# Relative-position rows spread in memory by one copy instead of four writes from SBUF

## The chip, the cores and the metric

The kernel runs on one core of a Trainium2 chip. The metric is the device time of one execution in microseconds (us). Lower is better.

## What is computed

One layer of a decoder trunk for 256 tokens of 2048 features: a normalisation, one combined projection into the queries, keys, values and gates of three token mixers (native sparse attention, stick-breaking attention, indexer-selected attention), their gated merge, a gated MLP with a causal convolution, a per-layer embedding gate, and a final normalisation. Of this the change touches only how the relative-position bias gets into SBUF. The reference adds a bias that depends on the distance of query and key to the logits of two of the mixers:

```python
def t5_bucket(dist):
    n = jnp.maximum(dist, 0)
    ...
    return jnp.where(n < max_exact, n, large)

bias = jnp.transpose(tab_gr[t5_bucket(dist)], (2, 3, 0, 1))
logits = jnp.einsum('bgrqd,bgkd->bgrqk', qb, kb).astype(jnp.float32) * scale + bias.astype(jnp.float32)
```

There are 12 heads with such a bias (8 and 4), and `tab` has 32 buckets for each.

## The kernel before

**Matrix products.** Weights come from memory in tiles of at most 1 MB, one DMA each on SP's queue, into the buffers `raw` (four). `load_w` (lines 114 to 129) makes two parts of each: `hi` on ACT (L125) and the rest `lo` on VectorE (L126), four buffers each, 1024 columns at a time. I call one such piece of work a split; it holds half of a weight tile. `gemm` (L137, L138) then runs a pair of matmuls for each of 16 blocks of 128 features, so a half tile is eight pairs. A feature tile (`feature_tiles`) is 16 pairs, ended by a fold: ACT copies half of the PSUM tile (L238), VectorE adds (L239), GpSimd scales (L240). A value tile (`value_tiles`, L290 to L292) takes four weight tiles.

**Foreground and background.** `tile_of` loads and splits the weights of the next tile before the epilogue of the last one is written down. The mixers are generators in the background: `pump()` advances each active generator by one `yield`, and takes up one waiting generator, after every feature tile (after every second weight tile of a value tile). The instruction order on each engine is then set by a scheduler from simulated times, so an instruction can stand earlier or later than its place in the program text. Every engine works its instructions off in order, and DMAs issued by an engine stand in that order too.

**The tile order around the change.** sbq (four feature tiles), sbk (four), sbv (one value tile of four weight tiles), then ikw, dckv, iq, dq and so on. `later(toeplitz())` stands behind sbq.

**The position rows.** `toeplitz` (lines 317 to 333) multiplies the table by a one-hot matrix (L319), which gives for each of 12 heads the 256 biases by distance, and writes them into `rrow`, 12 partitions of 384 numbers, the last 128 masked (L321, L322). A Toeplitz tile needs row p shifted by p. For this each head's row of 1536 bytes is written 128 times into the scratch tensor `scr` in memory, and `toe` reads it back with a step of 383 numbers from partition to partition, two heads in each of six DMAs (L330). The writes are four DMAs of three heads each, so out of three partitions (L326). Both are issued by ACT (`nc.scalar`). The stick-breaking part (`stick`) does not use `toe`; the first reader is `selected` (L440), after 240 us.

The parameters `prm` (L267) come in one DMA of 128 rows with 2508 numbers, 10,032 bytes each.

Of the kernel before, what the change touches and what calls it, by code (L numbers as in the profile page):

```python
# [11 lines left out]
F32 = mybir.dt.float32  # L12
F32R = mybir.dt.float32r

P = 128
S = 256
# [21 lines left out]
def trunk(ctx, tc, xT, pT, wf, wv, wg, wpa, wpb, wpc, wout, ck1, cv1, gmix, params, fg, fu, fd,  # L38
          plg, plp, out):
    nc = tc.nc  # L40
# [17 lines left out]
    def psa():  # L58
        return pa.tile([P, 512], F32, tag="pa", name="pa")
# [4 lines left out]
    def feat(name, dt=F32):  # L64
        return f2.tile([P, 512], dt, tag="f2", name=name)
# [4 lines left out]
    def tmp2(name):  # L70
        return wk.tile([P, 512], F32, tag="t2", name=name, bufs=4)

# [1 line left out]
    x_sb = big.tile([P, KT, S], F32, tag="x", name="x_sb")  # L74
    warm = cst.tile([P, 2], F32, tag="warm", name="warm")
    vec.memset(warm, 0.0)
# [33 lines left out]
    uk, uv, w2k, w2v = (par(n, 2) for n in ("wuk", "wuv", "ck2", "cv2"))  # L110
    cws = par("cw", NFF)

# [1 line left out]
    def load_w(src, cuts, cols):  # L114
        kt = sum(cuts)
        if first:
            raw = first.pop().rearrange("p (k c) -> p k c", c=cols)
        else:
            raw = wr.tile([P, 2048], F32, tag="raw", name="raw")[:, 0:kt * cols].rearrange("p (k c) -> p k c", c=cols)
            nc.sync.dma_start(raw, src)  # L120
        parts, k = [], 0
        for n in cuts:
            hi = wh.tile([P, 1024], F32R, tag="hi", name="hi")[:, 0:n * cols].rearrange("p (k c) -> p k c", c=cols)
            lo = wh.tile([P, 1024], F32R, tag="lo", name="lo")[:, 0:n * cols].rearrange("p (k c) -> p k c", c=cols)
            act(hi, raw[:, k:k + n, :], AF.Copy)  # L125
            vec.tensor_tensor(lo, raw[:, k:k + n, :], hi.bitcast(F32), op=ALU.subtract)  # L126
            parts.append((hi, lo, n))
            k += n
        return parts
# [43 lines left out]
            return r, rn, ps  # L173
        return spread

# [1 line left out]
    active, waiting = [], deque()  # L177

    def pump():
# [9 lines left out]
        while active or waiting:  # L189
            pump()  # L190

# [1 line left out]
    pending = []  # L193

    def flush():
# [13 lines left out]
    def later(*gens):  # L209
        then(lambda: waiting.extend(gens))  # L210

# [1 line left out]
    hs = []  # L213
    ssq4 = [tmp2("ssq4") for _ in range(2)]
    for k in range(KT):
# [27 lines left out]
    norm = []  # L243
# [3 lines left out]
    def feature_tiles(n, name):  # L247
        tiles = []

        def one(i):  # L250
            def evac(ps):
                if i % 2 == 0:
                    tiles.append(feat(name))
                fold_norm(tiles[-1][:, (i % 2) * 256:(i % 2) * 256 + 256], ps, norm[0])
                pump()

            def run(parts):
                ps = psg()
                gemm(ps, parts, hs)
                if norm:  # L260
                    evac(ps)
                    return
                early.append((evac, ps))
                if len(early) == 2:
                    early.insert(0, mixer_norm())
                elif len(early) == 4:
                    nc.sync.dma_start(prm, params)  # L267
                    norm.extend(early.pop(0)()[0:2])
                    for f, ps in early:
                        f(ps)  # L270
            return run

        for i in range(n):
            tile_of(wf[fidx[0]], (8, 8) if fidx[0] else (4, 4, 4, 4), 128, one(i))
            fidx[0] += 1
        return tiles
# [34 lines left out]
        split(o, ps[:, 0:256])  # L311
        return o

# [1 line left out]
    toes = []  # L315

    def toeplitz():
        pt = psa()
        mm(pt[0:12, 0:256], tabs, oh, start=True, stop=True)  # L319
        rrow = cst.tile([12, 384], F32, tag="rrow", name="rrow")  # L320
        nc.gpsimd.memset(rrow, NEG)  # L321
        vec.tensor_copy(rrow[:, 0:256], pt[0:12, 0:256])  # L322
        scr = nc.dram_tensor("scr", (12, P, 384), F32, kind="Internal").ap()
        yield
        for i in range(4):
            nc.scalar.dma_start(scr[3 * i:3 * i + 3], rrow[3 * i:3 * i + 3, None, :].to_broadcast([3, P, 384]))  # L326
            yield
        for i in range(6):
            t = feat("toe")
            nc.scalar.dma_start(t.rearrange("p (h k) -> p h k", h=2),  # L330
                                bass.AP(tensor=scr.tensor, offset=scr.offset + 127 + 2 * i * P * 384,
                                        ap=[[383, P], [P * 384, 2], [1, S]]))
            toes.append(t)

# [1 line left out]
    o_b, o_c, o_a = [], [], []  # L336

    def stick(h):
# [22 lines left out]
           skip_group_check=True)  # L361
        o_b.append(to_xs(ps, "ob"))

# [1 line left out]
    gates = cst.tile([P, 2, 24], F32, tag="gates", name="gates")  # L365
    wi = cst.tile([P, 2, 8], F32, tag="wi", name="wi")
    latent = {}
# [95 lines left out]
        if i == 1:  # L463
            o_c.append(to_xs(accs["c"], "oc"))

# [1 line left out]
    comp = {}  # L467

    def blocks(key, src, pe):
# [121 lines left out]
        if i == 1:  # L591
            o_a.append(to_xs(accs["a"], "oa"))

# [1 line left out]
    sbq = feature_tiles(4, "sbq")  # L595
    later(toeplitz())
    sbk = feature_tiles(4, "sbk")
    sbv = value_tiles(0, "sbv")
# [27 lines left out]
    then(drain)  # L626
    later(*(sparse(h, i) for h in range(8) for i in range(2)))

# [1 line left out]
    y, ys = [], []  # L630

    def gate_tile(parts):
# [66 lines left out]
    for n in range(KT):  # L699
        tile_of(wout[n], (8, 8), 128, lambda parts, n=n: out_tile(parts, n))  # L700

# [1 line left out]
    pre = {}  # L703

    def gate_up(parts, f):
# [102 lines left out]
    later(embed_inputs())  # L808
    ffn_down(NFF // CHUNK - 1, prev, True)

# [1 line left out]
    def ple_tile(parts, n):  # L812
        if n == 0:
            sums["f"] = wk.tile([P, S], F32, tag="ssq", name="ssq")
        pj = half(pps, n)
        ps = psg()
        if n == KT - 1:
            k = 0
            for hi, lo, c in parts:
                for j in range(c):  # L820
                    xh, xl = pxl[k][:, 0:256], pxl[k][:, 256:512]
                    for e, (w, x) in enumerate(((hi, xh), (hi, xl), (lo, xh))):
                        mm(ps[:, 0:256], w[:, j, :], x, start=k + e == 0, stop=k == KT - 1 and e == 2)  # L823
                    k += 1
            ple_evac(ps, pj, n)
            return
        gemm(ps, parts, pxl)
        if n == 0:
            sums["s"] = rstd_of([sums["q"]], D, "r1")
            sums["g"] = lambda: ple_evac(ps, pj, n)  # L830
            return
        if n == 1:
            sums["r"] = sums["s"]()[0]
            sums["g"]()
        ple_evac(ps, pj, n)
# [117 lines left out]
```

## Time and profile before

| | |
|---|---|
| median of 3 runs | 1672.39 us (1672.28 to 1672.94) |
| span of the profiled execution | 1670.0 us |
| TensorE busy | 1626.6 us, 97% of the span |
| VectorE, ACT, GpSimd busy | 68%, 53%, 10% |
| memory read / written | 299.94 MB / 4.46 MB |

The profiled execution's own time is not listed apart from its span; the median of the runs is 2.39 us longer than the span. The span runs from the first to the last instruction; PE is the matmul part of TensorE, PEld its weight load, DVE VectorE, POOL GpSimd, SP the engine that issues most DMAs; a q behind a name is the engine's own instruction queue. "Granted clock" is the share of TensorE's full clock.

### The profile page before, as it was taken

Reading aid. Unit: us, or ns where it says so; the run is one execution under the profiler, and the core shown is the slowest. Engines: PE = TensorE matmul, PEld = TensorE weight load, DVE = VectorE, ACT = ScalarE, POOL = GpSimd, SP = SyncE. Lnnn points to the kernel's source line nnn. Section 1 sums busy time; section 2 is a strip of 40 time slices with the busy share of each in tenths; the row PEclk is TensorE's granted clock in tenths of the full one; section 3 lists DMA queues with packets and bytes.
Section 4 is the critical chain, followed back from the end, with each engine's and each line's share of the span. In section 5 each row is a group of like instructions: output and inputs, shape, how many; then the busy total and the mean of one; then the engine's idle time right before and its main releaser. Section 6 shows DMA issues by size and latency. Waiting matters only on the chain.

```text
span 1670.0 us, 24647 instructions
## 1 busy us (share of the span) xinstructions
PE 1626.6 (97%) x9382; PEld 1418.8 (85%) x9382; DVE 1143.9 (68%) x1903; ACT 876.8 (53%) x1431; POOL 169.1 (10%) x177
## 2 busy tenths in 40 slices
PE   8499999999999999999999999999999999999996
PEld 6388888888888888888888888888888888889886
DVE  7145586776777666667777777666776677667775
ACT  5148455555565555555555555445554455446664
POOL 4001161210001110012100000000000000001122
PEclk7799999999999999999999999999999999999998
DMA  7265446554444555555555555565546655565551
GB/s 285 80 232 188 154 175 217 202 187 150 140 153 165 195 209 189 189 211 193 185 193 183 196 185 185 158 228 193 186 155 197 225 180 178 171 196 168 202 202 51
DMA packets 55074, 306.06 MB, mean 183 GB/s; under 512 B 5868, under 2 KB 9260, under 8 KB 27052
## 3 DMA queue, kind: packets, MB, share of 16 engines
q1 hardware_dynamic: 51552, 299.96, 52.2%
q10 hardware_dynamic: 3404, 4.52, 0.9%
q8 instruction: 74, 1.21, 0.3%
q14 instruction: 44, 0.36, 0.1%
HBM read 299.94 MB, written 4.46 MB: 182 GB/s over the span
## 4 chain that ended last, share of the span: by engine, by line
PE 95%; ACTq 2%; DVE 1%; ACT 0%; issue 0%; DVEq 0%
PE pg L137 58%; PE pg L138 29%; ACTq L326 2%; PE pg L292 1%; PE pg L290 1%; PE pg L291 1%; PE po L589 1%; PE po L501 0%; PE po L500 0%; PE po L585 0%; PE pg L823 0%; PE pa L543 0%; PE pa L544 0%; PE pa L576 0%; PE pa L154 0%; PE pa L412 0%
## 5 line engine op out<-in xcount | busy, mean ns | idle before, releaser
L126 DVE TENSOR_TENSOR lo<-raw,hi 128x1024 fp32r<-128x1024 f32 (+2 forms) x616 | 697.8, 1134 | 427.9 <-ACT hi L125 426.3
L125 ACT ACTIVATE hi<-raw 128x1024 fp32r<-128x1024 f32 (+2 forms) x616 | 602.3, 979 | 704.6 <-PE pg L137 455.8
L137 PE MATMUL pg<-h,hi 128*128 128x512 f32 x1328 | 482.6, 403 | 25.7 <-ACT hi L125 23.1
L137 PE MATMUL pg<-xf,hi 128*128 128x512 f32 x1408 | 488.7, 394 | 0.0
L138 PE MATMUL pg<-xf,lo 128*128 128x256 f32 x1408 | 389.9, 277 | 0.0
L138 PE MATMUL pg<-h,lo 128*128 128x256 f32 x1328 | 379.9, 286 | 3.7 <-DVE lo L126 3.6
L137 PEld LDWEIGHTS pg<-h,hi 128*128 128x128 f32 x1328 | 253.1, 191 | 87.0 <-ACT hi L125 24.1
L137 PEld LDWEIGHTS pg<-xf,hi 128*128 128x128 f32 x1408 | 264.0, 188 | 61.1
L138 PEld LDWEIGHTS pg<-xf,lo 128*128 128x128 f32 x1408 | 264.4, 188 | 0.1
L138 PEld LDWEIGHTS pg<-h,lo 128*128 128x128 f32 x1328 | 255.1, 192 | 8.0 <-DVE lo L126 6.3
L137 PE MATMUL pg<-f,hi 128*128 128x512 f32 x704 | 245.8, 394 | 0.0
L138 PE MATMUL pg<-f,lo 128*128 128x256 f32 x704 | 195.5, 278 | 0.0
L137 PEld LDWEIGHTS pg<-f,hi 128*128 128x128 f32 x704 | 132.1, 188 | 30.3
L678 POOL TENSOR_TENSOR ssq<-ssq,sqn 128x256 f32<-128x256 f32 x44 | 51.1, 1161 | 871.7 <-ACT sqn L677 867.2
L138 PEld LDWEIGHTS pg<-f,lo 128*128 128x128 f32 x704 | 132.4, 188 | 0.0
L137 PE MATMUL pg<-ys,hi 128*128 128x512 f32 x256 | 88.7, 393 | 0.0
L137 PE MATMUL pg<-xp,hi 128*128 128x512 f32 x240 | 83.8, 393 | 0.0
L240 POOL TENSOR_TENSOR gt<-fold,r 128x256 f32<-128x256 f32 x48 | 40.5, 845 | 358.7 <-DVE fold L239 336.7
L138 PE MATMUL pg<-ys,lo 128*128 128x256 f32 x256 | 70.8, 277 | 0.0
L138 PE MATMUL pg<-xp,lo 128*128 128x256 f32 x240 | 67.4, 281 | 0.0
L137 PEld LDWEIGHTS pg<-ys,hi 128*128 128x128 f32 x256 | 47.9, 187 | 11.0
L143 ACT ACTIVATE fold<-pg 128x256 f32<-128x256 f32 x151 | 55.1, 365 | 0.0
(257 smaller groups left out, 1675.2 us busy)
## 6 DMA issues: line engine op xcount, KB each, us to landing
raw<-in_wg_dram SPq DMA_DIRECT2D x48, 1024.0 KB, 4.8
raw<-in_fg_dram SPq DMA_DIRECT2D x44, 1024.0 KB, 4.9
raw<-in_fu_dram SPq DMA_DIRECT2D x44, 1024.0 KB, 4.8
raw<-in_fd_dram SPq DMA_DIRECT2D x64, 704.0 KB, 4.1
raw<-in_wf_dram SPq DMA_DIRECT2D x33, 1024.0 KB, 4.8
raw<-in_wout_dram SPq DMA_DIRECT2D x16, 1024.0 KB, 4.9
raw<-in_plg_dram SPq DMA_DIRECT2D x16, 1024.0 KB, 4.9
raw<-in_wv_dram SPq DMA_DIRECT2D x8, 1024.0 KB, 11.0
```

Of the source, the lines that this page charges most:

```text
L125: act(hi, raw[:, k:k + n, :], AF.Copy)
L126: vec.tensor_tensor(lo, raw[:, k:k + n, :], hi.bitcast(F32), op=ALU.subtract)
L137: mm(ps[:, 0:512], hi[:, j, :], xs[k][:, 0:512], start=k == 0, stop=last)
L138: mm(ps[:, 256:512], lo[:, j, :], xs[k][:, 0:256], start=False, stop=last, skip_group_check=True)
L143: act(t, ps[:, 256:512], AF.Copy)
L240: nc.gpsimd.tensor_tensor(dst, t, r, op=ALU.mult)
L290: mm(pss[t], xh, hi[:, j, :], start=k == 0, stop=False)
L291: mm(pss[t], xl, hi[:, j, :], start=False, stop=False)
L292: mm(pss[t], xh, lo[:, j, :], start=False, stop=k == KT - 1)
L326: nc.scalar.dma_start(scr[3 * i:3 * i + 3], rrow[3 * i:3 * i + 3, None, :].to_broadcast([3, P, 384]))
L589: mm(o, nv[c][:, b * 256 + g * 128:b * 256 + g * 128 + 128], pt_[:, s * 128:s * 128 + 128], start=False, stop=s == nb - 1)
L678: nc.gpsimd.tensor_tensor(ssq, ssq, t, op=ALU.add)
```

## The change

`scr` gets the layout (128, 12, 384) in place of (12, 128, 384). `rrow` is written once into a new tensor `row` in memory, 12 rows of 1536 bytes, and one DMA from memory to memory writes the 18,432 bytes of `row` 128 times into `scr`. The reads of `toe` have the same shape; a partition's row now lies 12 x 384 - 1 numbers behind that of the partition before. The generator has three yields ahead of the reads instead of five.

```diff
-        scr = nc.dram_tensor("scr", (12, P, 384), F32, kind="Internal").ap()
-        yield
-        for i in range(4):
-            nc.scalar.dma_start(scr[3 * i:3 * i + 3], rrow[3 * i:3 * i + 3, None, :].to_broadcast([3, P, 384]))
-            yield
+        row = nc.dram_tensor("row", (12, 384), F32, kind="Internal").ap()
+        scr = nc.dram_tensor("scr", (P, 12, 384), F32, kind="Internal").ap()
+        nc.scalar.dma_start(row, rrow)
+        yield
+        nc.scalar.dma_start(scr, row[None, :, :].to_broadcast([P, 12, 384]))
+        yield
+        yield
         for i in range(6):
             t = feat("toe")
             nc.scalar.dma_start(t.rearrange("p (h k) -> p h k", h=2),
-                                bass.AP(tensor=scr.tensor, offset=scr.offset + 127 + 2 * i * P * 384,
-                                        ap=[[383, P], [P * 384, 2], [1, S]]))
+                                bass.AP(tensor=scr.tensor, offset=scr.offset + 127 + 2 * i * 384,
+                                        ap=[[12 * 384 - 1, P], [384, 2], [1, S]]))
             toes.append(t)
```

From line 323 on the changed kernel's lines are numbered differently: the write of `row` is L325, the copy L327, the reads of `toe` L332 (L330 before).

Where these DMAs stand on ACT, in the stretch of the last sbq tiles. Before, the four writes of `scr`; a `hi<-raw` is a split, a `fold` the end of a feature tile, and DMAHW is a count of landed DMAs:

```order
L238 ACTIVATE fold<-pg 128x256 [waits PE_49]
L172 ACTIVATE r_360<-pa 128x256 [waits PE_49]
L326 DMA scr<-rrow 384x1x384 [waits DVE_49]
L326 DMA scr<-rrow 384x1x384
L326 DMA scr<-rrow 384x1x384 [waits DMAHW1_49]
L125 ACTIVATE hi<-raw 128x1024 [waits DMAHW3_49,PE_49,Activation_49]
L326 DMA scr<-rrow 384x1x384
L125 ACTIVATE hi<-raw 128x1024 [waits PE_49,Activation_49]
L238 ACTIVATE fold<-pg 128x256 [waits PE_49]
L125 ACTIVATE hi<-raw 128x1024 [waits DMAHW4_49,PE_49,Activation_49]
L125 ACTIVATE hi<-raw 128x1024 [waits DVE_49,PE_49]
```

and with the change:

```order
L238 ACTIVATE fold<-pg 128x256 [waits PE_49]
L172 ACTIVATE r_360<-pa 128x256 [waits PE_49]
L325 DMA row<-rrow 12x384 [waits DVE_49]
L125 ACTIVATE hi<-raw 128x1024 [waits DMAHW3_49,PE_49,Activation_49]
L125 ACTIVATE hi<-raw 128x1024 [waits PE_49,Activation_49]
L238 ACTIVATE fold<-pg 128x256 [waits PE_49]
L327 DMA scr<-row 128x4608 [waits DMAHW6_49]
L125 ACTIVATE hi<-raw 128x1024 [waits DMAHW4_49,PE_49,Activation_49]
L125 ACTIVATE hi<-raw 128x1024 [waits DVE_49,PE_49]
```

One small DMA stands in the place of the first three writes and none between the two splits; the copy follows behind the next fold and waits for the landing of `row`.

The reads of `toe` on ACT, before, at the end of the value tile:

```order
L125 ACTIVATE hi<-raw 128x1024 [waits DVE_49,PE_49]
L125 ACTIVATE hi<-raw 128x1024 [waits DMAHW7_49,DVE_49,PE_49]
L297 ACTIVATE sbv<-pg,r1n 128x512 [waits PE_49]
L125 ACTIVATE hi<-raw 128x1024 [waits DVE_49,PE_49]
L297 ACTIVATE sbv<-pg,r1n 128x512 [waits PE_49]
L330 DMA toe<-scr 128x2x256 x3
L330 DMA toe<-scr 128x2x256 [waits DMAHW1_49]
L330 DMA toe<-scr 128x2x256 [waits DMAHW2_49]
L330 DMA toe<-scr 128x2x256 [waits DMAHW1_49]
L125 ACTIVATE hi<-raw 128x1024 [waits DMAHW0_49,DVE_49,PE_49]
L125 ACTIVATE hi<-raw 128x1024 [waits DVE_49,PE_49]
```

and with the change, at the end of the sbk tiles:

```order
L125 ACTIVATE hi<-raw 128x1024 [waits DMAHW7_49,DVE_49,PE_49]
L125 ACTIVATE hi<-raw 128x1024 [waits DVE_49,PE_49]
L238 ACTIVATE fold<-pg 128x256 [waits PE_49]
L125 ACTIVATE hi<-raw 128x1024 [waits DMAHW1_49,DVE_49,PE_49]
L332 DMA toe<-scr 128x2x256 [waits DMAHW0_49]
L332 DMA toe<-scr 128x2x256 x4
L332 DMA toe<-scr 128x2x256 [waits DMAHW2_49]
L238 ACTIVATE fold<-pg 128x256 [waits PE_49]
L125 ACTIVATE hi<-raw 128x1024 [waits DVE_49]
```

They have moved ahead of the fold of the last sbk tile, behind the first half of the second weight tile of sbv; the first of them waits for the landing of `scr`, the sixth for that of a weight tile.

## Rows read from the trace of the kernel before

**Rows 1.** The page: the chain that ended last by engine, and two groups of instructions

```profile
PE 95%; ACTq 2%; DVE 1%; ACT 0%; issue 0%; DVEq 0%
...
L126 DVE TENSOR_TENSOR lo<-raw,hi 128x1024 fp32r<-128x1024 f32 (+2 forms) x616 | 697.8, 1134 | 427.9 <-ACT hi L125 426.3
...
L143 ACT ACTIVATE fold<-pg 128x256 f32<-128x256 f32 x151 | 55.1, 365 | 0.0
```

**Rows 2.** Table of stretches; stretch first, its length, then the engines as named

```profile
core 0: us, PE busy (x) PEld busy (x) DVE busy (x) ACT busy (x) POOL busy (x), PEclk, DMA share, GB/s
50.50:69.50 19.00, 0.20 (x3) 0.03 (x1) 0.05 (x1) 1.06 (x1) 0.00 (x0) 0.63 0.18 48
69.50:86.40 16.90, 12.41 (x36) 9.63 (x37) 7.12 (x8) 5.63 (x8) 3.31 (x2) 0.60 0.43 132
86.40:200.00 113.60, 113.60 (x635) 98.44 (x634) 58.60 (x78) 67.89 (x91) 10.44 (x14) 1.00 0.55 193
200.00:1600.00 1400.00, 1400.00 (x8179) 1226.83 (x8179) 1004.05 (x1703) 744.95 (x1231) 120.97 (x129) 1.00 0.54 186
```

**Rows 3.** Timeline of ACT and its queue: start and length in us, then the work

```profile
39.73 28.51 ACTq L326 DMA_DIRECT2D scr<-rrow  x3
...
68.38 9.47 ACTq L326 DMA_DIRECT2D scr<-rrow  x1
...
118.99 0.92 ACTq L330 DMA_DIRECT2D toe<-scr  x2
...
119.94 2.81 ACTq L330 DMA_DIRECT2D toe<-scr  x4
```

**Rows 4.** Line L326: its DMA issues on ACT's queue, shortest, median and longest

```profile
L326 ACTq DMA_DIRECT2D scr<-rrow x4: 1344/10874/14814, 39.7 to 68.4; - x4
```

**Rows 5.** Waits of TensorE from 39 to 90 us: total us, times, longest

```profile
PE pg L137 <- ACT hi L125: 22.1, 2, 18.8
PE pg L138 <- DVE lo L126: 1.2, 2, 0.8
```

**Rows 6.** Timeline of TensorE, single matmuls around the stall

```profile
39.91 0.40 PE L137 MATMUL pg<-h,hi 128*128 128x512 f32 x1
...
50.16 0.40 PE L137 MATMUL pg<-h,hi 128*128 128x512 f32 x1
...
71.11 0.63 PE L137 MATMUL pg<-h,hi 128*128 128x512 f32 x1
...
74.95 0.63 PE L137 MATMUL pg<-h,hi 128*128 128x512 f32 x1
...
86.42 0.39 PE L137 MATMUL pg<-h,hi 128*128 128x512 f32 x1
```

**Rows 7.** Timeline of SP's queue: the issue of the parameters

```profile
11.96 0.33 SPq L267 DMA_DIRECT2D prm<-in_params_dram  x1
```

**Rows 8.** DMA issues: count, size of one, median us from issue to landing

```profile
raw<-in_wf_dram SPq DMA_DIRECT2D x33, 1024.0 KB, 4.8
...
pre<-in_gmix_dram SPq DMA_DIRECT2D x1, 72.0 KB, 1.9
```

**Rows 9.** Timeline of ACT after the stall: two weight splits in a row

```profile
91.44 1.06 ACT L125 ACTIVATE hi<-raw 128x1024 fp32r<-128x1024 f32 x1 [1.76 <-PE pg L137]
...
94.27 1.06 ACT L125 ACTIVATE hi<-raw 128x1024 fp32r<-128x1024 f32 x1 [1.50 <-PE pg L137]
```

**Rows 10.** DMA from 0 to 40 us: slices of 1 us, and SP's queue

```profile
DMA  0189689999999999999999975997999961799200
GB/s 0 21 158 320 215 240 313 324 277 231 377 402 418 418 426 467 426 410 426 448 443 411 411 144 147 401 418 180 426 418 401 385 262 49 164 393 410 82 0 0
...
q1 hardware_dynamic: 3168, 11.84, 81.2%
```

**Rows 11.** DMA from 39.7 to 119 us: ACT's queue, and value-tile loads

```profile
q10 hardware_dynamic: 1548, 2.36, 11.5%
...
raw<-in_wv_dram SPq DMA_DIRECT2D x4, 1024.0 KB, 11.6
```

## The prediction

> **What bounds the kernel now.** I read the page first, then a table of stretches, then what the gap in it waits for, then the transfers.
>
> On the page TensorE carries 95% of the chain that ended last; the only other entry of weight is ACT's own queue with 2% [rows 1]. The table of stretches shows where the missing share lies [rows 2]: from 200 to 1600 us TensorE is busy for all of 1400 us at a granted clock of 1.00, and already from 86.4 us it has no idle time. In between it nearly stands still: from 50.5 to 69.5 us it has 0.20 us of work, and up to 86.4 us it is idle for another 4.5 us and its granted clock is 0.60.
>
> The ACT timeline shows the cause [rows 3]. The first three writes of scr (L326) hold ACT's queue from 39.73 for 28.51 us; after one weight split the fourth holds it from 68.38 for 9.47 us. Of the four issues the shortest took 1.34 us, the longest 14.81 [rows 4]. ACT issues its DMAs in order with its arithmetic, and all weight splits (L125, hi<-raw) stand behind them. TensorE runs on with the splits already made until about 50.5 us and then waits twice for hi, 18.8 us the longer time [rows 5]. The transfer is narrow too: in the stretch of the stall the DMA engines are busy for a share of 0.18, about 3 of 16 [rows 2], and each write of scr copies 1536-byte rows out of three partitions.
>
> So the question is not how many bytes move, but how long ACT's queue is held, and whether anything new holds it.
>
> **What the stall is worth.** At the full clock a pair of matmuls (L137 with L138) starts every 0.3535 us: from 39.91 to 50.16 there are 29 steps [rows 6]. The next pair would have started at 50.52. The full pace returns with the pair at 86.42. Between them stand 18 pairs (36 of the 36 to 39 matmuls that the two stretches list [rows 2]): 35.90 - 18 x 0.3535 = **29.5 us** lost. Of it 22.1 + 1.2 = 23.3 us are waits for hi and lo [rows 5], and some 5 us come from pairs at the lower of the two clock levels (1.2 and 2.4 GHz), which take 0.64 us each (71.11 to 74.95 in six steps [rows 6]). If TensorE is fed throughout, it never idles there, so both parts go. More than 29.5 us cannot be had here: from 86.4 to 1600 us TensorE has no idle time [rows 2], and neither the first 39 us nor the end are touched.
>
> **The change, part by part.** *Removed:* four writes of scr on ACT's queue. *Added:* one write of row (12 rows of 1536 bytes, 18 KB), one copy of it in memory into 128 rows of 18,432 bytes (2.36 MB, as much as before), and a wait ahead of each of the next two readers. *Moved:* the six reads of toe, from behind the value tiles to between two splits, four feature tiles earlier in time.
>
> *The write of row.* It is issued at about 39.75, where the first write of scr stood. Nothing like it is in the trace; the nearest rows are an issue of 0.33 us for 128 rows [rows 7] and a landing after 1.9 us for 72 KB [rows 8]. Its reader stands behind two splits and a fold. Splits run one per 2.83 us when TensorE paces them [rows 9]; TensorE begins the tile sbq3 at 39.1, so they come at 41.9 and 44.8, the fold ends near 46.2, and the copy is issued at **46.2**. The row has 6 us to land in and needs about 2. Cost: nothing.
>
> *The issue of the copy.* Bounds: 0.33 us, which prm took for 128 rows of 10,032 bytes [rows 7], and 14.81, the longest issue of an old write [rows 4]. I take 0.33, as prm's form is nearest: 128 rows, 8 pieces for each of 16 engines, where an old write has 128 pieces for each of three. At the other end TensorE, fed until 56.1 by the split of 44.8 and four half tiles of 2.83 us, would lose some 6 us.
>
> *The copy's own time.* Here ACT can be held again: the first read of toe waits for scr. Per engine it is 2.36 MB / 16 = 147 KB. The busiest loads ran 11.84 MB in 81.2% of 16 x 40 us, 22.8 GB/s per engine [rows 10]; the old writes of scr ran 2.36 MB in 11.5% of 16 x 79.3 us, 16.2 GB/s [rows 11]. That gives 6.5 to 9.1 us alone. Beside it the weights take 65.5 KB per engine in each 5.66 us, 11.6 GB/s, and leave 11.2 of 22.8: 13 us, with a landing about **15 us** after the issue. Both ends of the copy lie in memory, and all its rows read the same 18 KB; at half the pace it would be 26 to 28 us. I take 15, being nearest to the load rows, which reach 426 to 467 GB/s in some slices of 1 us [rows 10].
>
> A rule of the Trainium skill speaks against this: HBM Reference, "Specifications (TRN2)", gives a core an effective 358 GB/s. If reads and writes of the copy, 4.72 MB, had to share that with the weights, it would last about 27 us by an estimate from that page of the Trainium skill, and the sum would be 1647 in place of 1643. The trace does not agree with it as a limit, by the slices just named.
>
> *Is that soon enough?* Between the copy and the reads of toe stand seven splits and three folds; the last split ahead of them starts at 64.6 (41.9 + 8 x 2.83), so they are due at 65.6, 19.4 us after the copy is issued. If ACT were held there, TensorE would run dry four halves after that split, at 75.8. Ahead of the next split come six reads (0.92 + 2.81 = 3.7 us [rows 3]), a fold (0.4), the split (1.1) and the subtraction behind it (1.1) [rows 1, 9]: scr must land by 69.5, **23 us** after the issue. With 15 us there are 8 us to spare, and at 28 us the loss is 5 us.
>
> *The moved reads* cost ACT the same 3.7 us. In the old place they cost TensorE nothing (no idle time from 119 us on [rows 2]), and the new one comes before the stick-breaking part loads ACT. The sixth read also waits for a weight load issued near 53, landed by then. Cost: nothing, within the 11 us that TensorE is fed ahead. *SP's queue* is not reordered there; its loads share the engines with the copy. A load issued at 47 is due at 64.6; it usually lands in 4.8 us [rows 8], and with all of the copy ahead of it in some 18, which just fits. Value-tile loads that took 11.6 us [rows 11] left no idle time from 86.4 to 119 [rows 2]. Cost: nothing.
>
> **Sum.** 1670.0 - 29.5 = 1640.5 us of span. The median of the runs is 1672.39, 2.39 above that span; I keep this distance: **1642.9 us**.
>
> **The rivals.**
> *The copy is late but spread* (8%): reading one 18 KB row from all engines, or writing to the memory it reads, halves or quarters the pace, and ACT waits at the first read of toe. For it speaks that no copy from memory to memory is in the trace; against it, the 8 us to spare. A landing 28 to 50 us after the issue costs 5 to 27 us: 1648 to 1670. With a wait that long little of the gain is left.
>
> *The copy is narrow, and ACT is held longer than now* (5%, the slower side). If it ran on one engine, 2.36 MB at 16.2 to 22.8 GB/s would last 104 to 146 us; less the 23 of cover, ACT's wait at the first read of toe would cost 81 to 123 us on top of 1642.9: 1724 to 1766. It is slower than before from a landing 23 + 29.5 = 52 us after the issue (45 GB/s). The old writes, with three rows outermost, show that it can happen: a DMA share of 0.18 [rows 2]. Against it: 128 rows are outermost on both sides now, as in the weight loads, during which the share reaches 0.9 and more in whole slices [rows 10]. The Trainium skill, DMA: Bandwidth & Descriptors, "Why a DMA increments its semaphore by 16 and not by 1", has the number of engines as the largest up to 16 that divides both slowest dimensions, 3 for the old writes and 16 for the copy. By that rule, with which the share of 0.18 agrees, I give this rival 5% and not more.
>
> *The weights are late instead* (3%): pieces of 18 KB in each engine's way push the loads back more than 18 us; TensorE waits a few us for raw: 1645 to 1650.
>
> *The reordering bites, or the stall stays* (2%): the order of all engines is written by a scheduler from simulated times, and further down it differs in how background work is interleaved; but a new wait of 29 us is hard to see where TensorE has none now. About 1672.
>
> **The numbers.** Forecast 82%: 1640.5 to 1647, likeliest 1642.9. The range takes in the late issue and the smaller part of the late copy and ends at 1650. A measurement of this kernel can tell about 0.2% (3.3 us) from no change; faster 0.93, the same 0.02, slower 0.05.
>
> **What would show it.** Right: no DMA issue of ACT over 1 us between 39 and 70 us, the copy's packets on all engines, the first toe issue near 65.6 without a wait, TensorE busy at clock 1.00 from 40 us on. Wrong: a long issue at the copy or at the first toe, idle time of TensorE near 76 us on hi, or waits of ACT for raw.

## The result, and the profile after

The kernel takes 1641.47 us (median; 1640.79 to 1642.48 in 4 runs) where the kernel before took 1672.34: a ratio of 0.982, 95% interval 0.981 to 0.983. That is 30.9 us less. The forecast was 1642.9 with a range of 1640 to 1650. The profiled execution took 1642.48 us with a span of 1640.7.

The page after: TensorE's share of the chain has gone from 95% to 98%, and ACT's queue [rows 1] has left it.

```profile
span 1640.7 us, 24645 instructions
...
PE 98%; DVE 0%; ACT 0%; DVEq 0%; issue 0%
```

The table of stretches, with the columns of [rows 2]: TensorE is busy without a gap from 38 to 1570 us, at a granted clock of 1.00. From 50.5 to 69.5 us it has 19.00 us of work, where it had 0.20 before.

```profile
38.00:50.50 12.50, 12.50 (x71) 10.25 (x70) 5.96 (x8) 5.06 (x7) 3.88 (x4) 1.00 0.51 166
50.50:69.50 19.00, 19.00 (x109) 16.42 (x108) 9.00 (x10) 7.24 (x10) 2.22 (x3) 1.00 0.87 295
69.50:86.40 16.90, 16.90 (x76) 14.00 (x75) 8.41 (x8) 7.64 (x8) 0.75 (x1) 1.00 0.76 279
86.40:200.00 113.60, 113.60 (x659) 98.05 (x659) 71.10 (x130) 69.91 (x100) 17.81 (x25) 1.00 0.45 158
200.00:1570.00 1370.00, 1370.00 (x8007) 1201.92 (x8006) 977.10 (x1637) 729.94 (x1206) 110.78 (x115) 1.00 0.55 187
```

The timeline of ACT and its queue, against [rows 3]: the write of row takes 0.58 us, the copy 0.57, the six reads of toe 3.65, and the splits go on between them. After the sixth read the next split starts at 69.72.

```profile
40.73 0.58 ACTq L325 DMA_DIRECT2D row<-rrow  x1
...
46.07 0.57 ACTq L327 DMA_DIRECT2D scr<-row  x1
...
65.74 1.07 ACT L125 ACTIVATE hi<-raw 128x1024 fp32r<-128x1024 f32 x1 [1.49 <-PE pg L137]
65.74 3.65 ACTq L332 DMA_DIRECT2D toe<-scr  x6
...
69.72 1.05 ACT L125 ACTIVATE hi<-raw 128x1024 fp32r<-128x1024 f32 x1
```

The DMA answer for 46 to 61 us, in which the copy runs (queue q10 is ACT's, q1 SP's; packets, MB, share of 16 engines; in the issues, us to landing): the copy lands 14.1 us after its issue and thus at 60.2, 5.5 us before anyone asks for it. Its pieces took 0.529 x 15 x 16 = 127 us of engine time for 2.36 MB, 18.6 GB/s per engine. Value-tile loads beside it took 10.2 us to land, and TensorE did not notice.

```profile
q10 hardware_dynamic: 144, 2.36, 52.9%
q1 hardware_dynamic: 270, 1.94, 36.7%
...
raw<-in_wv_dram SPq DMA_DIRECT2D x3, 1024.0 KB, 10.2
scr<-row ACTq DMA_DIRECT2D x1, 2304.0 KB, 14.1
```

How much came from where can be read from one line late in both kernels, the squares of the output features (before, then after; the last figures are the first and the last start):

```profile
L677 ACT ACTIVATE sqn<-x_sb x44: 398/418/421, 744.8 to 1652.1; 128x256 f32<-128x256 f32 x44
```

```profile
L679 ACT ACTIVATE sqn<-x_sb x44: 399/417/421, 716.3 to 1623.7; 128x256 f32<-128x256 f32 x44
```

The last split ahead of the stall, and the first result of the value tile, in ACT's timeline (before, then after):

```profile
38.14 1.06 ACT L125 ACTIVATE hi<-raw 128x1024 fp32r<-128x1024 f32 x1 [1.77 <-PE pg L137]
...
118.30 0.69 ACT L297 ACTIVATE sbv<-pg,r1n 128x512 f32<-128x512 f32 x1 [1.21 <-PE pg L292]
```

```profile
39.15 1.06 ACT L125 ACTIVATE hi<-raw 128x1024 fp32r<-128x1024 f32 x1 [1.77 <-PE pg L137]
...
89.82 0.69 ACT L297 ACTIVATE sbv<-pg,r1n 128x512 f32<-128x512 f32 x1 [1.21 <-PE pg L292]
```

The split started at 38.14 us before and, as the first stage happened to run, at 39.15 after. From there to the last of these squares it is 1613.96 us before and 1584.55 after: 29.4 us less. All of it is already there at the end of the value tile, which came 80.16 us behind that split before and comes 50.67 us behind it now. The late start costs 1.0 us. The last stretch, behind the squares, is 0.9 us shorter: TensorE's granted clock there was 0.62 before and 0.71 after, and it was busy for 4.88 and 4.15 us.

### The profile page after: what moved, and what is told of

The parts are those of the page before. It is cut to its first block, busy times and chain, and to the rows that moved or that the text cites. A ratio compares the mean times of both kernels' runs of the same rounds, so it can differ in the third digit from the quotient of the medians.

```text
span 1640.7 us, 24645 instructions
## 1 busy us (share of the span) xinstructions
PE 1620.6 (99%) x9382; PEld 1414.9 (86%) x9382; DVE 1143.9 (70%) x1903; ACT 876.4 (53%) x1431; POOL 166.4 (10%) x177
## 4 chain that ended last, share of the span: by engine, by line
PE 98%; DVE 0%; ACT 0%; DVEq 0%; issue 0%
PE pg L137 59%; PE pg L138 30%; PE pg L290 1%; PE pg L292 1%; PE pg L291 1%; PE po L591 1%; PE po L503 0%; PE po L502 0%; PE po L587 0%; PE pg L825 0%; PE pa L545 0%; PE pa L546 0%; PE pa L578 0%; PE pa L414 0%; PE pa L154 0%; PE pa L794 0%
```

## The experiments

The theory: ACT's queue was held because each of three engines was given 512 pieces, the weight splits stood behind the held issues, and TensorE ran dry. The rivals: the narrow, slow transfer itself starves TensorE by delaying the weights; the new source in memory, or the new size of the pieces, is what helps; the loss goes with the amount written. Ten kernels were run; each was timed against the kernel before on its own chip (1671 us).

### The same writes from another queue

Against the kernel before:

```diff
-            nc.scalar.dma_start(scr[3 * i:3 * i + 3], rrow[3 * i:3 * i + 3, None, :].to_broadcast([3, P, 384]))
+            nc.gpsimd.dma_start(scr[3 * i:3 * i + 3], rrow[3 * i:3 * i + 3, None, :].to_broadcast([3, P, 384]))
```

> The kernel before, with its four three-row writes of scr issued by GpSimd (nc.gpsimd) in place of ACT; same bytes, same pieces, same three engines wide. Held queue: ACT's queue is free, so the 29 us are gone as in the change; left is only a wait of ACT at the first read of toe if the narrow writes land after about 92 us (they landed near 116 us before): 1641 to 1656 us. Narrow transfer (three busy DMA engines slow the weights, and that starves TensorE): nothing changes, 1665 to 1673 us.

Measured: 1645.6 us, ratio 0.985 (0.983 to 0.986). The DMA issues of scr (shortest, median, longest in ns), a wait of ACT in its timeline, and GpSimd's queue q0 from 42 to 110 us:

```profile
L326 POOL DMA_DIRECT2D scr<-rrow x4: 1059/1064/1227, 42.5 to 45.8; - x4
```

```profile
71.19 2.01 ACT L125 ACTIVATE hi<-raw 128x1024 fp32r<-128x1024 f32 x2 [7.67 <-DMA raw<-in_wv_dram]
```

```profile
q0 software_dynamic: 2816, 2.39, 30.1%
```

GpSimd takes each write in about 1.1 us, ACT's queue is free, and 25.6 of the 30 us are gone. One line of the program was changed, but more than the queue came of it, and here the expectation was wrong. The transfer was not three engines wide: 30.1% of 16 x 68 us is 327 us of engine time, and three engines have only 204 in that stretch. Nor were the pieces the same: by the size counts of the two pages, 1536 packets of 512 B to 2 KB are gone and 516 of 2 to 8 KB have come. So this run speaks for the queue, and neither for the pieces nor for a narrow transfer. The wider transfer does some harm: ACT waits up to 7.7 us for value-tile weights, and the kernel stays 4 us behind the change.

### Narrow copies from memory

Against the kernel before, with the rows copied to memory first as in the change:

```diff
+        row = nc.dram_tensor("row", (12, 384), F32, kind="Internal").ap()
+        nc.scalar.dma_start(row, rrow)
+        yield
         for i in range(4):
-            nc.scalar.dma_start(scr[3 * i:3 * i + 3], rrow[3 * i:3 * i + 3, None, :].to_broadcast([3, P, 384]))
-            yield
+            nc.scalar.dma_start(scr[3 * i:3 * i + 3], row[3 * i:3 * i + 3, None, :].to_broadcast([3, P, 384]))
```

> The row is written to memory once as in the change, but spread by four copies of three rows each (scr in its old layout, 128 pieces of 1536 bytes for each of three engines), on ACT. Held queue: ACT is held again, some 6 us later in the program, for 25 to 40 us; TensorE waits as before: 1662 to 1678 us. If taking the source from memory instead of SBUF is what helps: 1640 to 1645 us.

Measured: 1653.6 us, ratio 0.990 (0.988 to 0.992), between the two expectations. ACT's timeline, TensorE's wait, and the transfer from 45 to 93 us:

```profile
45.18 3.39 ACTq L328 DMA_DIRECT2D scr<-row  x2
...
48.71 18.07 ACTq L328 DMA_DIRECT2D scr<-row  x2
66.88 1.06 ACT L125 ACTIVATE hi<-raw 128x1024 fp32r<-128x1024 f32 x1 [17.13 <-issue]
```

```profile
PE pg L137 <- ACT hi L125: 8.7, 1, 8.7
```

```profile
q10 hardware_dynamic: 1496, 2.28, 12.7%
```

ACT is held again, so a source in memory does not free it. But it is held for some 21 us and not 38. The theory had the cause of the hold and missed a second one for its length: from memory the same pieces drain faster. A piece took 0.127 x 48 x 16 us / 1496 = 65 ns, where it took 95 ns from SBUF (11.5% of 16 x 79.3 us for 1536 pieces [rows 11]).

### One write of all twelve rows

Against the kernel before, with the reads of toe as far behind as in the change:

```diff
-        for i in range(4):
-            nc.scalar.dma_start(scr[3 * i:3 * i + 3], rrow[3 * i:3 * i + 3, None, :].to_broadcast([3, P, 384]))
-            yield
+        nc.scalar.dma_start(scr, rrow[:, None, :].to_broadcast([12, P, 384]))
+        yield
+        yield
```

> The kernel before, with one write of all twelve rows from SBUF in place of four of three rows: no row in memory, no copy from memory to memory; 128 pieces of 1536 bytes for each of twelve engines. Held queue, by pieces per engine: like the first old write (1.34 us) it is taken without a hold, 1.3 to 5 us of ACT, inside the 11 us that TensorE is fed ahead: 1640 to 1643 us, the same as the change. Held by the total of 1536 small pieces: ACT is held some 30 us as before: 1665 to 1675 us.

Measured: 1650.9 us, ratio 0.988 (0.986 to 0.990), neither of the two. ACT's timeline, the transfer from 39 to 77 us, and TensorE's wait:

```profile
39.87 1.42 ACTq L325 DMA_DIRECT2D scr<-rrow  x1
...
64.41 1.06 ACT L125 ACTIVATE hi<-raw 128x1024 fp32r<-128x1024 f32 x1 [1.44 <-PE pg L137]
77.14 3.00 ACTq L330 DMA_DIRECT2D toe<-scr  x6
```

```profile
q10 hardware_dynamic: 1548, 2.36, 42.4%
```

The same answer for 46 to 50 us:

```profile
q10 hardware_dynamic: 188, 0.29, 68.9%
```

```profile
PE pg L290 <- ACT hi L125: 6.1, 1, 6.1
```

The issue takes 1.42 us: 1536 pieces are no trouble if they are spread. From 46 to 50 us the share of this queue was 68.9%, just under 12 of 16 engines, which is 128 pieces for each of twelve. What was not expected is that the write lands only near 77 us, 37 us after its issue. ACT waits at the first read of toe, and TensorE 6.1 us for a split. A piece took 0.424 x 38 x 16 us / 1536 = 168 ns, more than the 95 ns of the narrow writes.

### A copy three times as tall

Against the change; nothing is added to what is read from it:

```diff
-        scr = nc.dram_tensor("scr", (P, 12, 384), F32, kind="Internal").ap()
+        scr = nc.dram_tensor("scr", (3 * P, 12, 384), F32, kind="Internal").ap()
...
-        nc.scalar.dma_start(scr, row[None, :, :].to_broadcast([P, 12, 384]))
+        nc.scalar.dma_start(scr, row[None, :, :].to_broadcast([3 * P, 12, 384]))
```

> The change, with a copy three times as tall (384 rows of 18,432 bytes, 7.1 MB; toe reads the first 128). Cover of 23 us: the copy lands about 38 us after its issue, so ACT waits at the first read of toe until about 84 us, and TensorE, fed until about 73 us in this order, loses 15 to 25 us: 1656 to 1667 us. If the copy's length does not matter at all: 1640 to 1644 us.

Measured: 1654.4 us, ratio 0.990 (0.988 to 0.992). The copy's landing, ACT's timeline, and TensorE's wait:

```profile
scr<-row ACTq DMA_DIRECT2D x1, 6912.0 KB, 33.4
```

```profile
46.27 0.57 ACTq L327 DMA_DIRECT2D scr<-row  x1
...
79.67 3.77 ACTq L332 DMA_DIRECT2D toe<-scr  x6
83.50 2.00 ACT L125 ACTIVATE hi<-raw 128x1024 fp32r<-128x1024 f32 x2 [14.66 <-issue]
```

```profile
PE pg L290 <- ACT hi L125: 10.1, 1, 10.1
```

It landed after 33.4 us, not 38, and the time is 1.6 us below the range that was expected. The loss against the change is 12.9 us. Of it TensorE waits 10.1 us for the split that stands behind the reads of toe, and by the prediction's sum this wait is 33.4 - 23 = 10.4: the cover of 23 us holds. The rest fits the clock, which was granted at 0.81 from 80 to 100 us, where TensorE worked for 15.4 us. A late copy thus costs 2.5 us more than the first rival of the prediction said. The order is not quite that of the change: here the reads stand behind the last sbk fold and one split earlier, so it is the cover of this order that was measured.

The run also tells pieces from bytes. This copy gives each of 16 engines 432 KB in 24 pieces, and its issue takes 0.57 us; the first two old writes give each of three engines 384 KB in 256 pieces, and the second is held. Nor is it the number of DMAs on the way: the six reads of toe are issued within 3.77 us, before the first of them can have landed (5.3 us at the least).

### One and two of the four old writes

Against the kernel before. With fewer writes the generator also has fewer yields, so the reads of toe stand further ahead:

```diff
-        for i in range(4):
+        for i in range(1):
...
-                                bass.AP(tensor=scr.tensor, offset=scr.offset + 127 + 2 * i * P * 384,
+                                bass.AP(tensor=scr.tensor, offset=scr.offset + 127 + (i % 2) * P * 384,
```

> The kernel before with only the first of the four writes of scr; the reads of toe take heads 0 to 2 for all, so the bias of nine heads is another one. Held queue: the first write was taken in 1.34 us, and it alone holds nobody; it lands before the first read of toe near 65 us: 1640 to 1644 us. Loss in proportion to the bytes or pieces written: a quarter of 29 us stays, about 1649 us.

Measured: 1642.5 us, ratio 0.983 (0.981 to 0.985). ACT's timeline:

```profile
39.56 1.36 ACTq L326 DMA_DIRECT2D scr<-rrow  x1
...
68.71 3.34 ACTq L330 DMA_DIRECT2D toe<-scr  x6
```

One write is taken in 1.36 us and holds nobody. It lands late, near 68.7 us, where the expectation had it before 65. The reads of toe, due near 65.6, wait some 3 us for it, which is inside the cover.

```diff
-        for i in range(4):
+        for i in range(2):
...
-                                bass.AP(tensor=scr.tensor, offset=scr.offset + 127 + 2 * i * P * 384,
+                                bass.AP(tensor=scr.tensor, offset=scr.offset + 127 + (2 * i % 4) * P * 384,
```

> The kernel before with the first two of the four writes; the reads of toe take heads 0 to 3 for all. Held queue: the second write holds ACT for some 15 us, to 56 us; TensorE, fed until 50.5 us, waits some 6 us and runs its first pairs at the lower clock: 1648 to 1653 us. Loss in proportion: half of 29 us, about 1656 us.

Measured: 1659.8 us, ratio 0.993 (0.991 to 0.995). ACT's timeline and TensorE's waits:

```profile
40.00 16.20 ACTq L326 DMA_DIRECT2D scr<-rrow  x2
...
74.65 14.46 ACTq L330 DMA_DIRECT2D toe<-scr  x6
```

```profile
PE pg L137 <- ACT hi L125: 6.5, 1, 6.5
PE pg L290 <- ACT hi L125: 4.8, 1, 4.8
```

The hold is there as expected, 16.20 us for both issues, and so is TensorE's wait of 6.5 us for it. The expectation missed by 7 us since it left out the landing: the reads of toe hold ACT for 14.46 us more, and TensorE waits again, 4.8 us. In the kernel before these reads stood 44 us later [rows 3], so there only the hold counted. The rival by the amount written named 1656, which is nearer in number; but with one write it has a quarter of the loss left, and there nothing was left.

### The size of the pieces, and the source

The change with unused numbers between the heads, so that rows no longer join:

```diff
-        scr = nc.dram_tensor("scr", (P, 12, 384), F32, kind="Internal").ap()
+        scr = nc.dram_tensor("scr", (P, 12, 400), F32, kind="Internal").ap()
...
-        nc.scalar.dma_start(scr, row[None, :, :].to_broadcast([P, 12, 384]))
+        nc.scalar.dma_start(scr[:, :, 0:384], row[None, :, :].to_broadcast([P, 12, 384]))
```

> The change, with 16 unused numbers behind each head's row in scr, so that the copy has 96 pieces of 1536 bytes for each of 16 engines in place of 8 of 18,432; source and width stay. If a slow source in SBUF made the single write of twelve rows late: pieces from memory took 66 ns each in the narrow copies, 96 of them 6.3 us, and the copy lands within 20 us: 1640 to 1643 us, the same as the change. If small pieces are what is slow: it lands after 30 us and more, ACT waits at the first read of toe, 1647 to 1655 us.

Measured: 1641.8 us, ratio 0.982 (0.981 to 0.984), as the change. The copy, from 45 to 63.5 us:

```profile
q10 hardware_dynamic: 1552, 2.36, 38.3%
...
scr<-row ACTq DMA_DIRECT2D x1, 2304.0 KB, 17.2
```

The pieces are twelve times as many, 0.383 x 18.5 x 16 us / 1552 = 73 ns each, and the copy lands after 17.2 us and not 14.1. That is inside the cover, so the tall pieces of the change are worth 3 us of landing and nothing in time.

The one write of twelve rows, with memory as its source:

```diff
-        nc.scalar.dma_start(scr, rrow[:, None, :].to_broadcast([12, P, 384]))
+        row = nc.dram_tensor("row", (12, 384), F32, kind="Internal").ap()
+        nc.scalar.dma_start(row, rrow)
+        yield
+        nc.scalar.dma_start(scr, row[:, None, :].to_broadcast([12, P, 384]))
```

> The single write of twelve rows, twelve engines wide with 128 pieces of 1536 bytes for each, with memory as its source (row written once, as in the change). Slow source in SBUF: it lands within 20 us of its issue, and the time is that of the change, 1640 to 1643 us. Small pieces or the width of twelve slow: as with the source in SBUF, 37 us to land, about 1650 us or, issued 6 us later, up to 1657 us.

Measured: 1642.6 us, ratio 0.983 (0.981 to 0.985). The transfer, and ACT's timeline:

```profile
q10 hardware_dynamic: 1538, 2.35, 35.9%
```

```profile
45.57 0.89 ACTq L328 DMA_DIRECT2D scr<-row  x1
...
65.52 2.85 ACTq L333 DMA_DIRECT2D toe<-scr  x5
```

A piece takes 0.359 x 18.5 x 16 us / 1538 = 69 ns where it took 168 from SBUF, with the same twelve rows outermost and so the same 128 pieces per engine. TensorE waits for nothing from 25 to 1600 us. So with the shape held, the source decides.

### Is it SBUF, or where the rows lie in it?

The table is multiplied with its columns four apart, so that the rows come out on partitions 0, 4, 8 to 44, and the one write of twelve rows takes them from there:

```diff
-        mm(pt[0:12, 0:256], tabs, oh, start=True, stop=True)
-        rrow = cst.tile([12, 384], F32, tag="rrow", name="rrow")
+        tpad = cst.tile([32, 48], F32, tag="tpad", name="tpad")
+        nc.gpsimd.memset(tpad, 0.0)
+        vec.tensor_copy(tpad[:, 0:48:4], tabs)
+        mm(pt[0:48, 0:256], tpad, oh, start=True, stop=True)
+        rrow = cst.tile([48, 384], F32, tag="rrow", name="rrow")
...
-        nc.scalar.dma_start(scr, rrow[:, None, :].to_broadcast([12, P, 384]))
+        nc.scalar.dma_start(scr, rrow[0:48:4, None, :].to_broadcast([12, P, 384]))
```

> The single write of twelve rows from SBUF, with the rows on partitions 0, 4, 8 to 44 in place of 0 to 11 (the table is multiplied with columns four apart; a small memset and a copy are added). Same pieces, same twelve engines, source still in SBUF. Adjacent partitions share a narrow way out of SBUF: each way now feeds two engines at most and not four, a piece takes well under the 168 ns of the adjacent rows, the write lands before the first read of toe near 65 us, and the time is that of the change, 1640 to 1643 us. SBUF as such is the slow source, however the rows lie: it lands near 77 us as before, 1649 to 1653 us.

Measured: 1643.8 us, ratio 0.984 (0.982 to 0.985), 0.8 us above the upper end that was expected. The transfer from 39 to 66 us, and ACT's timeline:

```profile
q10 hardware_dynamic: 1548, 2.36, 29.3%
```

```profile
40.22 1.41 ACTq L328 DMA_DIRECT2D scr<-rrow  x1
...
66.09 3.77 ACTq L333 DMA_DIRECT2D toe<-scr  x6
```

A piece takes 0.293 x 27 x 16 us / 1548 = 82 ns in place of 168, though it still comes out of SBUF. The write lands at 66 us, just when it is wanted, and not at 77. What slowed it was that its rows lay on neighbouring partitions. The Trainium skill, SBUF — State Buffer, "Door 1: The DMA port swizzle", has groups of four partitions share one port towards the DMA engines; by that rule rows 0 to 11 leave by three ports and rows 0, 4 to 44 by eight. The two piece times agree with it in direction; the ports themselves appear in no trace.

The four narrow writes with the same placing:

```diff
-            nc.scalar.dma_start(scr[3 * i:3 * i + 3], rrow[3 * i:3 * i + 3, None, :].to_broadcast([3, P, 384]))
+            nc.scalar.dma_start(scr[3 * i:3 * i + 3], rrow[12 * i:12 * i + 12:4, None, :].to_broadcast([3, P, 384]))
```

> The kernel before, four writes of three rows, with the rows four partitions apart as in the run beside it. The queue still gets 512 pieces for each of three engines, so ACT is still held, but for a shorter time if its engines drain them faster. Adjacent partitions slow: near the narrow copies from memory (held some 18 to 22 us in all): 1650 to 1658 us. SBUF as such slow: held 38 us, 1668 to 1674 us.

Measured: 1656.5 us, ratio 0.991 (0.989 to 0.993). ACT's timeline, and the transfer from 39 to 90 us:

```profile
41.38 14.25 ACTq L329 DMA_DIRECT2D scr<-rrow  x3
...
55.77 7.54 ACTq L329 DMA_DIRECT2D scr<-rrow  x1
```

```profile
q10 hardware_dynamic: 1444, 2.20, 11.5%
```

ACT is held for 14.25 + 7.54 = 21.8 us in place of 28.51 + 9.47 = 38.0 [rows 3], and a piece takes 0.115 x 51 x 16 us / 1444 = 65 ns in place of 95. So the hold of the old kernel has two factors: how many pieces each engine is given, and how fast they drain.

This run answers the rival of the narrow transfer as well. By 90 us 1444 packets had gone out, of 1548 as in the kernel before, so the narrow writes ran on long after ACT came free at 63.3 us. The stretch from 66 to 100 us, with the columns of [rows 2]:

```profile
66.00:100.00 34.00, 34.00 (x163) 28.81 (x164) 18.82 (x19) 14.33 (x17) 5.55 (x5) 0.95 0.68 243
```

TensorE had no idle time there. Once ACT's queue was free, the narrow transfer starved nobody.

## Why the prediction was right

*What the stall is worth.* Forecast 29.5 us, measured 29.4 over the same work. The step that carries the forecast (18 pairs in 35.9 us, priced at the full clock) held, and so did its bound: nothing more was gained behind the value tile.

*The write of row.* Forecast at 39.75 and free; it came at 40.73 (the whole stage was 1.0 us late), and its reader did not wait.

*The copy's issue.* Forecast 0.33 us at 46.2, measured 0.57 at 46.07. The issue of prm was the right row to choose, the old writes the wrong one. That the start agrees so well is luck: the stage ran 1.0 us late, and the sum had the copy behind the fold, while the trace has it beside the split ahead of that fold (46.01) and before the fold starts (46.98).

*The copy's own time.* Forecast a landing after 15 us, measured 14.1. This too is partly luck, since two terms were off in opposite directions: the copy ran at 18.6 GB/s per engine and not 22.8, and the weights beside it took 1.94 MB in 15 us, 8.1 GB/s per engine, and not 11.6. The 27 us that I had estimated from the Trainium skill, HBM Reference, "Specifications (TRN2)", did not come. The trace does not agree with 358 GB/s as a limit: the copy's 4.72 MB, read and written, and the 1.94 MB of weights are 444 GB/s over these 15 us. Nor does that section of the Trainium skill call it one, since it has a core that streams alone well above it. The lower row that I had as a bound, 16.2 GB/s per engine of the old writes, was a property of neighbouring rows in SBUF, which I had taken for one of the transfer: from rows four partitions apart the same pieces ran at 1536 / 65 ns = 23.6 GB/s.

*The cover.* Forecast 23 us from issue to need. The copy of three times the height, landing after 33.4 us and costing 12.9, confirms it to a few us, in an order that differs by one split and one fold.

*The moved reads and the weights.* Reads due at 65.6 came at 65.74 without a wait and took 3.65 us against 3.7. The start agrees by the same luck: they came beside the split ahead of them, which started 1.1 us late, and not behind it. Value-tile loads landed in 10.2 us, well inside the 18 us allowed.

*Around the span.* I carried 2.39 us over from the kernel before, the median of its runs less the span of one of them. In each of the four runs after, time and span lie 1.8 us apart, and the profiled one was the slowest: together the 1.4 us by which the median lies under the forecast.

*The rivals.* None came true. A narrow copy is no disaster at three engines: it costs 12 us, and the kernel stays faster than before. On one engine, as the rival had it, none was run. A late copy was produced on purpose and cost 12.9 us, where the rival's price is 10.4. Weights that come late, though by another cause, were seen with GpSimd's writes: 1645.6 us, inside the 1645 to 1650 of that rival.

Left open is how many pieces an engine's queue takes before the issuing engine is held. The runs only bound it: 128 for each of twelve engines were taken in 1.42 us; a second 128 for each of three were not from SBUF (16.20 us for both), while from memory both were taken in 3.39 us.

## What to carry to other kernels

An engine that computes should not issue DMAs that give a few DMA engines hundreds of small pieces: as on ACT here, the issue itself holds the engine, and everything in its order behind it. Count pieces per DMA engine ahead of bytes, spread the outermost dimension over all engines, and keep the reader of the result further behind than the landing. For a row that is copied many times, take the source from memory, or from partitions that lie apart.

## What the runs showed of the hardware that I had not expected

Copying 1536-byte rows out of SBUF took 168 ns a piece from twelve neighbouring partitions, 82 ns from twelve that lie four apart, and 69 ns from memory, with twelve rows outermost each time and beside value-tile loads. And a copy from memory to memory, 128 times the same 18,432 bytes, ran at 18.6 GB/s per engine; at three times the height it landed its 6912 KB in 33.4 us. Whether the one source row was in its way no run tells.
